# Block 1's key products by feature block, with re-laid first parameters

## The chip, the cores and the metric

The kernel runs on one core of a Trainium2 chip. The metric is the device time of one execution in microseconds, taken as the median of several runs. Beside it stands one profiled execution, whose trace gives every instruction with its start, its duration and what it waited for. Engines: PE is TensorE, with PEld its weight loads; DVE is VectorE, ACT ScalarE, POOL GpSimd, and SP issues the transfers.

## What is computed

Three transformer blocks run over 256 tokens of width 1024: `first_block`, then two blocks of a second model. The part that matters here is the opening of the first one. Two streams, the tokens `x` and a context `ctx`, are normalised and modulated with parameters that come from conditions through a wide matrix, and then projected:

```
sh_a, sc_a, ... = split(silu(c)     @ w_ada + b_ada, 6)      # w_ada: 1024 x 6144
csh_a, csc_a,.. = split(silu(c_ctx) @ w_ada + b_ada, 6)
hc = modulate(rmsnorm(ctx, norm_mix), csh_a, csc_a)          # h * (1 + scale) + shift
hx = modulate(rmsnorm(x,   norm_mix), sh_a,  sc_a)
u  = h @ w_in        # split into qk, v, o, gates, and q, k, v of an attention
```

For the context only keys, values and gates are used; for the tokens all columns. A gated linear recurrence (mLSTM) with four heads and a window attention follow, then an output projection, a feed-forward stage, and the two blocks of the second model, which have parameters of their own (`w_ada_2`).

## The kernel before

All activations lie feature-major: a stream is eight tiles of 128 features by 256 tokens. A product in single precision is made of three fast ones (`mm3`): both operands are split into a rounded `hi` and a rest `lo`, and hi*hi, hi*lo and lo*hi are summed in one accumulation bank (L285 to L287). `load_w` loads 512 KB of weights into a raw tile, casts it to `hi` on ACT (L270) and forms `lo` on DVE or POOL (L273). `proj_fm` makes one 128-feature output block at a time, with the weights stationary and 256 tokens of one stream moving; `proj_tm` makes token-major outputs (values, gates), 272 or 384 columns wide, with the activations stationary.

Work is issued through three lanes, each with its own rings: main (raw tiles `wrm`, five accumulation banks `ppm`), fill (`wrf`, two banks `ppf`) and side (`wra`, two raw tiles, one bank `ppa`). The instructions are written in program order, and a planner orders them when the kernel is built: each engine takes, among what is ready by the planner's own estimate, what comes first in the program. On the chip each engine then keeps that order. SP issues all loads, in one order of its own.

The start runs so. `cond_silu` prepares the conditions. `ada_first` computes shift and scale of both streams in two halves `q` of the feature range, each from eight raw tiles of 512 KB that are borrowed from the three lanes' rings: for each raw tile `ada_mm` (L427) runs four matmuls in four column groups of the array, for both conditions at once. `ada_cols` copies the bank, transposes it in two f32 matmuls against the identity (L435), and two small DVE instructions and a scaling with `norm_mix` finish each half. The streams and the constants are loaded between the raw tiles, after the fourth of them. `rms_bc` squares a stream on ACT (L445, L450), adds on DVE (L448), sums over features with one-column f32 matmuls (L463), takes the root on POOL and spreads the result by f32 matmuls against the identity (L472). `norm_mod` then scales (L516), adds the shift on ACT (L521, L524) and forms `hi` and `lo` per tile of 256 tokens (L522, L523, L525).

`block1` follows: the second value projection with the gates (`win_tm1`, L756 to L759), the early parameters of block 2 (`early`: sixteen raw tiles of `wada20` on the side lane), and then, woven with the gates' chain, four key blocks (`ev_k`: convolution and SiLU), the first value projection (`win_tm0`), the attention's key block (`ev_ka`) and twelve blocks of queries and output gates for the tokens alone (`B1ORD`). The gates' chain begins after four steps of the weave (`pause(4)`); its first matmuls are L851 to L853.

Of the kernel before, what the change touches and what calls it, by code (L numbers as in the profile page):

```python
# [9 lines left out]
F32 = mybir.dt.float32  # L10
# [8 lines left out]
P = 128  # L19
# [5 lines left out]
NKEEP = 5472  # L25
# [3 lines left out]
B1ORD = (*range(9, 13), *range(5, 9), *range(13, 17))  # L29
# [30 lines left out]
for _n, _c in (  # L60
    ("norm_mix", 8), ("norm_ffn", 8), ("final_norm", 8), ("final_norm_w_2", 8),
    ("b_ada", 48), ("b_ada_20", 48), ("b_ada_21", 48),
    ("conv_qk", 32), ("mlstm_norm", 4), ("conv_ffn", 88),
    ("conv_ssd", 48), ("ssd_norm_w", 4), ("ret_gn_w", 4), ("q_norm", 6), ("kv_norm", 2),
    ("gate_b", 16), ("sink", 8), ("dt_bias", 16), ("a_log", 16), ("ssd_d", 8), ("decay", 16), ("iota", 8),
):
    _col(_n, _c)
# [15 lines left out]
def drive(gen):  # L83
    for _ in gen:
        pass
# [76 lines left out]
class Kern:  # L162
# [51 lines left out]
    def load_consts(self):  # L214
        nc = self.nc
        nc.sync.dma_start(self.cols, self.A["cols"])
        nc.sync.dma_start(self.cst, self.A["cst"])
# [6 lines left out]
        nc.vector.tensor_scalar(self.bm[:, 3], self.m["lt"], BIG, None, op0=MUL)  # L224

# [117 lines left out]

    def ada_first(self, W, cond, bcol, mid, use):

        nc, L = self.nc, self.side
        Wv = W[:, 0:2048].rearrange("p (a b) -> p a b", a=2)
        M, F, S = self.main, self.fill, self.side
        for q, raws in enumerate(((M, F, S, M, F, M, S, F), (S, F, S, F, S, F, S, F))):
            ps = L.ps()  # L350
            for k in range(8):
                R = raws[k]
                raw = self.tile([P, 1024], F32, "wr" + R.name, R.raw)
                nc.sync.dma_start(raw.rearrange("p (a b) -> p a b", a=2),
                                  Wv[k * P:(k + 1) * P, :, q * 512:(q + 1) * 512])
                if q == 0 and k == 3:
                    mid()
                self.ada_mm(ps, cond, raw, k)
            pt = self.ada_cols(L, ps)
            b0, _ = COLS[bcol]  # L360
            halves = []
            for a in range(2):
                dst = self.one([P, 2, 4], F32, f"ada_m{q}{a}")
                src = ap_of(pt[:, 64 * a:64 * a + 1], [(1, 2), (32, 2), (128, 2)])
                bo = b0 + 8 * a + 4 * q
                bsrc = ap_of(self.cols[:, bo:bo + 1], [(0, 2), (2, 2), (1, 2)])
                nc.vector.tensor_tensor(dst.rearrange("p c (n j) -> p c n j", j=2), src, bsrc, op=ADD)
                halves.append(dst)
            use(q, *halves)

    def ada(self, W, cond, bcol, out, groups):

        nc, L = self.nc, self.side
        for q in groups:
            ps = L.ps()
            for k in range(8):
                raw = self.tile([P, 1024], F32, "wra", L.raw)
                nc.sync.dma_start(raw, W[k * P:(k + 1) * P, q * 1024:(q + 1) * 1024])
# [60 lines left out]
    def sumsq(self, L, xs):  # L439
# [3 lines left out]
        for i, x in enumerate(xs):  # L443
# [6 lines left out]
            nc.scalar.activation(sq, x, AF.Square)  # L450
# [50 lines left out]
    def norm_mod(self, L, xs, a, sh, out, n=D, slots=None, scale=None):  # L501
# [10 lines left out]
        def start(k):  # L512
            hi, lo = slots(k) if slots else (L.s1(F32R), L.s1(F32R))
            out.append((hi, lo))
            t = L.s1()
            nc.vector.scalar_tensor_tensor(t, xs[k], a[k], bc, op0=MUL, op1=MUL)  # L516
            if sh is None:
                nc.scalar.copy(hi, t)
                return lambda: (nc.gpsimd if k % 2 else nc.vector).tensor_sub(lo, t, hi)
            if k % 2:  # L520
                nc.scalar.activation(t, t, AF.Identity, bias=sh[k])  # L521
                nc.scalar.copy(hi, t)  # L522
                return lambda: nc.gpsimd.tensor_sub(lo, t, hi)  # L523
            nc.scalar.activation(hi, t, AF.Identity, bias=sh[k])  # L524
            return lambda: nc.vector.scalar_tensor_tensor(lo, t, sh[k], hi, op0=ADD, op1=SUB)  # L525
# [187 lines left out]
    def block1(self, xs, hc, hx, ad, early, early2, late):  # L713
# [79 lines left out]
        def ev_x(mb, *a):  # L793
# [892 lines left out]
    def run(self, out, parts=("b1", "l0", "l1")):  # L1686
# [14 lines left out]
        if "b1" in parts:  # L1701
            c1 = self.load_stream("c1T", [M.s2() for _ in range(4)])
            sh, am, hc, hx = [[], []], [[], []], [], []
            norms = [self.norm_mod(M.on(Fl), c1, am[1], sh[1], hc), self.norm_mod(M.on(Fl), xs, am[0], sh[0], hx)]

            def streams():
                self.load_stream("xT", x2)
                self.load_consts()
                for _ in range(3):
                    for g in norms:  # L1710
                        next(g)

            def half(q, a, b):
                for c in range(2):
                    t = self.keep(4)
                    nc.vector.scalar_tensor_tensor(t, b[:, c], 1.0, self.col("norm_mix", 4 * q, 4), op0=ADD, op1=MUL)
                    am[c] += cl(t)
                    sh[c] += cl(a[:, c])

# [198 lines left out]
```

## Time and profile before

| | us |
|---|---|
| median of 3 runs | 1579.48 |
| lowest and highest run | 1576.5 and 1580.1 |
| the profiled execution, device time | 1574.8 |
| its span in the trace | 1573.0 |

The span is the time from the first to the last instruction in the trace; the device time of that execution has 1.8 us more around it. Busy times of TensorE are those of pipelined matmuls, whose ends are modelled, so durations of neighbours overlap; the distance between two starts is what one of them costs in a stream. The granted clock is given as a share of the full 2.4 GHz.

### The profile page before, as it was taken

To read this page: it belongs to the slowest core of one execution; us is meant where nothing else is said; L and a number is where in the kernel's file an instruction comes from. 1 tells how busy PE (TensorE), PEld (TensorE's weight loads), DVE (VectorE), ACT (ScalarE), POOL (GpSimd) and SP (SyncE) were. 2 spreads that over 40 slices of the span, in tenths; PEclk is the share of its full clock that TensorE was granted. 3 is DMA by queue.
4 is the path that set the end of the run, shared out by engine and by line. 5 is a ranking of instruction groups with operands and counts; after the bars stand their busy time and mean duration, and the time that the engine had idled before them with its cause. 6 is when DMAs were issued, how large, how long until landed. Compare 5 with 4: busy or idle time off the path is not lost.

```text
span 1573.0 us, 28294 instructions
## 1 busy us (share of the span) xinstructions
PE 1506.4 (96%) x10518; PEld 1330.7 (85%) x10518; DVE 1133.2 (72%) x2369; ACT 796.1 (51%) x1707; POOL 391.1 (25%) x373
## 2 busy tenths in 40 slices
PE   6899999999999998999999999999998999999997
PEld 3598867879999987888899888888898865899997
DVE  4457588579999946777775348988685775687776
ACT  3444546576545464645464323322366556566563
POOL 0102136231213263476572001101012112010000
PEclk9799999999999997999999999999999999999999
DMA  9856651456777763434245335688443340355663
GB/s 333 276 184 201 229 185 44 134 173 227 246 262 258 244 212 117 127 88 147 80 155 168 94 98 211 213 287 283 153 125 117 95 134 1 95 175 176 186 180 116
DMA packets 81386, 268.49 MB, mean 171 GB/s; under 512 B 9056, under 2 KB 10720, under 8 KB 80992
## 3 DMA queue, kind: packets, MB, share of 16 engines
q1 hardware_dynamic: 80672, 266.16, 52.3%
q8 instruction: 82, 1.34, 0.3%
q10 hardware_dynamic: 576, 0.52, 0.1%
q14 instruction: 56, 0.46, 0.1%
HBM read 265.60 MB, written 1.05 MB: 170 GB/s over the span
## 4 chain that ended last, share of the span: by engine, by line
PE 78%; DVE 8%; issue 6%; DMA 5%; ACT 2%; POOL 1%; SPq 0%; POOLq 0%; DVEq 0%; ACTq 0%
PE t_ppm L285 17%; PE t_ppm L286 17%; PE t_ppm L287 17%; PE t_ppf L285 4%; PE t_ppf L286 4%; PE t_ppf L287 4%; PE t_ppa L427 2%; PE t_ppm L1644 2%; DVE t_wlm L273 1%; PE t_ppm L1048 1%; PE t_ppf L1059 1%; DMA t_wra<-in_wada 1%; DMA t_wrm<-in_wdown 1%; PE t_ppm L1077 1%; PE t_ppm L972 1%
## 5 line engine op out<-in xcount | busy, mean ns | idle before, releaser
L270 ACT CAST t_whm<-t_wrm 128x512 fp32r<-128x512 f32 (+2 forms) x588 | 348.2, 598 | 400.7 <-PE t_ppm L286 308.3
L273 DVE TENSOR_TENSOR t_wlm<-t_wrm,t_whm 128x512 fp32r<-128x512 f32 (+3 forms) x551 | 402.4, 736 | 159.4 <-ACT t_whm L270 153.0
L285 PE MATMUL t_ppm<-t_g1m,t_whm 128*128 128x256 f32 x952 | 271.8, 291 | 0.0
L286 PE MATMUL t_ppm<-t_g1m,t_whm 128*128 128x256 f32 x952 | 269.3, 286 | 0.1
L287 PE MATMUL t_ppm<-t_g1m,t_wlm 128*128 128x256 f32 x952 | 267.4, 285 | 0.8 <-DVE t_wlm L273 0.8
L285 PEld LDWEIGHTS t_ppm<-t_g1m,t_whm 128*128 128x128 f32 x952 | 181.4, 192 | 4.9 <-issue 4.1
L286 PEld LDWEIGHTS t_ppm<-t_g1m,t_whm 128*128 128x128 f32 x952 | 182.3, 192 | 3.7 <-issue 2.8
L287 PEld LDWEIGHTS t_ppm<-t_g1m,t_wlm 128*128 128x128 f32 x952 | 181.4, 192 | 3.4 <-issue 1.7
L273 POOL TENSOR_TENSOR t_wlf<-t_wrf,t_whf 128x512 fp32r<-128x512 f32 (+1 forms) x92 | 118.0, 1291 | 193.9 <-ACT t_whf L270 184.2
L417 DVE SCALAR_TENSOR_TENSOR t_junk<-t_wra,t_sc 128x1024 bf16<-128x1024 f32 x120 | 151.1, 1262 | 18.5 <-DMA t_wra<-in_wada 14.0
L286 PE MATMUL t_ppm<-t_h8m,t_whm 128*128 128x512 f32 (+2 forms) x448 | 159.6, 357 | 1.9 <-DVE t_h8m L525 1.9
L285 PE MATMUL t_ppm<-t_h8m,t_whm 128*128 128x512 f32 (+1 forms) x448 | 158.6, 357 | 2.7 <-ACT t_h8m L524 2.7
L287 PE MATMUL t_ppm<-t_h8m,t_wlm 128*128 128x512 f32 (+2 forms) x448 | 159.2, 357 | 0.0
L270 ACT CAST t_whf<-t_wrf 128x512 fp32r<-128x512 f32 (+2 forms) x148 | 83.3, 574 | 107.3 <-PE t_ppf L286 73.3
L286 PE MATMUL t_ppm<-t_part,t_whm 128*128 128x258 f32 (+1 forms) x400 | 114.0, 285 | 0.0
L287 PE MATMUL t_ppm<-t_part,t_wlm 128*128 128x258 f32 (+1 forms) x400 | 113.6, 284 | 0.0
L285 PE MATMUL t_ppm<-t_part,t_whm 128*128 128x258 f32 (+1 forms) x400 | 113.3, 284 | 0.0
L285 PE MATMUL t_ppm<-t_g2m,t_whm 128*128 128x256 f32 x352 | 98.9, 283 | 0.6 <-ACT t_whm L270 0.5
L287 PE MATMUL t_ppm<-t_g2m,t_wlm 128*128 128x256 f32 x352 | 98.5, 283 | 0.8 <-DVE t_wlm L273 0.8
L286 PE MATMUL t_ppm<-t_g2m,t_whm 128*128 128x256 f32 x352 | 98.6, 282 | 0.0
L286 PEld LDWEIGHTS t_ppm<-t_h8m,t_whm 128*128 128x128 f32 (+1 forms) x448 | 83.9, 187 | 15.4 <-DVE t_h8m L525 2.3
L285 PEld LDWEIGHTS t_ppm<-t_h8m,t_whm 128*128 128x128 f32 x448 | 83.1, 187 | 16.2 <-ACT t_h8m L524 2.9
(542 smaller groups left out, 3521.9 us busy)
## 6 DMA issues: line engine op xcount, KB each, us to landing
t_wrm<-in_wup SPq DMA_DIRECT2D x132, 512.0 KB, 3.7
t_wra<-in_wada SPq DMA_DIRECT2D x102, 512.0 KB, 5.0
t_wrm<-in_w_fm SPq DMA_DIRECT2D x30, 512.0 KB, 3.6
t_wra<-in_wada20t SPq DMA_DIRECT2D x24, 512.0 KB, 4.6
t_wrf<-in_w_fm SPq DMA_DIRECT2D x20, 512.0 KB, 4.7
t_wrf<-in_wd SPq DMA_DIRECT2D x24, 384.0 KB, 3.9
t_wrm<-in_win_fm SPq DMA_DIRECT2D x17, 512.0 KB, 3.6
t_wrm<-in_wdown SPq DMA_DIRECT2D x16, 512.0 KB, 3.9
```

The costliest lines, as they stand in the source:

```text
L270: nc.scalar.copy(hi[:, :c1 - c0], raw[:, c0:c1])
L273: eng.tensor_sub(lo[:, :c1 - c0], raw[:, c0:c1], hi[:, :c1 - c0])
L285: mm(ps, ah, bh, start=start, stop=False)
L286: mm(ps, ah, bl, start=False, stop=False)
L287: mm(ps, al, bh, start=False, stop=stop)
L417: nc.vector.scalar_tensor_tensor(self.tile([P, D], BF16, "junk", 1), raw, 1.0, rows[:, c], op0=MUL, op1=MUL, accum_out=out[:, c, i:i + 1])
L427: self.nc.tensor.matmul(ps[32 * c:32 * c + 32, :T], cond[:, 32 * k:32 * (k + 1)], raw[:, c * T:(c + 1) * T], start=k == 0, stop=k == 7, ti ...
L972: nc.tensor.matmul(po[:, d * T:d * T + 129], Wt[d][c][:, sl], vm[c][:, h], start=i == 0, stop=i == len(keys) - 1)
L1048: nc.tensor.transpose(pp[:, j * T + t * P:j * T + (t + 1) * P], Ps[t][:, c * P:(c + 1) * P], self.m["ident"])
L1059: nc.tensor.matmul(po[j * 64:(j + 1) * 64, :T], v[j][c], pts[j][c // 2][:, (c % 2) * T:(c % 2 + 1) * T], start=c == 0, stop=c == 3, tile_p ...
L1077: nc.tensor.matmul(ps, q[:, t * P:(t + 1) * P], kall, start=True, stop=False)
L1644: nc.tensor.matmul(ps, q, K[0:96, hd], start=True, stop=True)
```

## The change

The first parameters are computed by feature block. The 2048 columns of shift and scale are laid out anew on the host (`wada1s`), so that for each of the eight feature blocks of 128 there are two tiles of 128 x 1024, with rows of 4 KB. `ada_block` runs both through one bank: column group c takes the condition's k = c and k = 4 + c, and two matmuls against a small selecting matrix (`sel`, two columns) sum the four groups and turn the result into columns. The raw tiles have a ring of their own, `wrq`, with five buffers. The weights of the five key blocks (four for the recurrence, one for the attention) are laid out by input feature (`win_k`, 128 x 640 for each).

`front` loads the context and the token stream first, then the column table and the identity. Squares and sums of both streams are formed (part of the second's squares on POOL), one root and four broadcasts serve both. Then, for each feature block k: its parameters, its weights, both streams scaled and split into one operand of 512 columns (`hw`, sixteen buffers), and fifteen products into five banks that stay open over all eight k. The other constants are loaded at k = 1. `block1` gets the five full banks and empties them, then goes on with the value projection as before; the key blocks leave the weave.

```diff
-        nc.sync.dma_start(self.cols, self.A["cols"])
-        nc.sync.dma_start(self.cst, self.A["cst"])
+        nc.sync.dma_start(self.cst[:, P:], self.A["cst"][:, P:])
...
+    def load_first(self):
+        self.nc.sync.dma_start(self.cols, self.A["cols"])
+        self.nc.sync.dma_start(self.cst[:, :P], self.A["cst"][:, :P])
...
-    def ada_first(self, W, cond, bcol, mid, use):
...
+    def ada_block(self, W, cond, bcol, fb, ncol):
         nc, L = self.nc, self.side
+        ps = L.ps()
+        for g in range(2):
+            raw = self.tile([P, 1024], F32, "wrq", 5)
+            nc.sync.dma_start(raw, W[:, g * 1024:(g + 1) * 1024])
+            for c in range(4):
+                k = 4 * g + c
+                nc.tensor.matmul(ps[32 * c:32 * c + 32, :T], cond[:, 32 * k:32 * (k + 1)], raw[:, c * T:(c + 1) * T],
+                                 start=g == 0, stop=g == 1, tile_position=(0, 32 * c))
+        sb = L.s1()
+        nc.vector.tensor_copy(sb, ps[:, :T])
+        pt = self.fill.ps()
+        for j in range(2):
+            nc.tensor.matmul(pt[:, 2 * j:2 * j + 2], sb[:, j * P:(j + 1) * P], self.col("sel", 0, 2), start=True, stop=True)
+        o, _ = COLS[bcol]
+        t, a = self.keep(4), self.keep(2)
+        v = lambda x: x.rearrange("p (j c) -> p j c", j=2)
+        nc.vector.tensor_tensor(v(t), v(pt[:, 0:4]), ap_of(self.cols[:, o + fb:o + fb + 1], [(8, 2), (0, 2)]), op=ADD)
+        nc.vector.scalar_tensor_tensor(a, t[:, 2:4], 1.0, ap_of(self.col(ncol, fb), [(0, 2)]), op0=ADD, op1=MUL)
+        return a, t[:, 0:2]
+
+    def front(self, cond, streams, loads, h):
+        nc, M, Fl, A = self.nc, self.main, self.fill, self.A
+        loads[0]()
+        loads[1]()
+        self.load_first()
+        with self.soon():
+            ps = Fl.ps()
+            for s, xs in enumerate(streams):
+                acc, sq = self.sumsq(M, xs, s)
+                nc.vector.tensor_add(acc, acc, sq)
+                for t in range(2):
+                    nc.tensor.matmul(ps[:, 2 * s + t:2 * s + t + 1], acc[:, t * P:(t + 1) * P], self.ones[:, 0:1],
+                                     start=True, stop=True)
+            v = M.sm(4)
+            nc.vector.tensor_scalar(v, ps[:, 0:4], 1.0 / D, EPS, op0=MUL, op1=ADD)
+            r = self.rsqrt(M, v, 4)
+            bc = Fl.ps()
+            for t in range(4):
+                nc.tensor.matmul(bc[:, t * P:(t + 1) * P], ap_of(r[:, t:t + 1], [(0, P)]), self.m["ident"],
+                                 start=True, stop=True)
+        pss = [M.ps() for _ in range(5)]
+        for k in range(8):
+            a, sh = self.ada_block(A["wada1s"][k], cond, "b_ada", k, "norm_mix")
+            w = self.load_w(M, A["win_k"][k], 640, P)
+            for s, xs in enumerate(streams):
+                sl = slice(s * T, (s + 1) * T)
+                c = 1 - s
+                self.mod_one(M, k, xs[k], a[:, c:c + 1], sh[:, c:c + 1], bc[:, sl], h[k][0][:, sl], h[k][1][:, sl])()
+            if k == 1:
+                self.load_consts()
+            for b in range(5):
+                wh, wl = w(b)
+                self.mm3(pss[b], wh, wl, h[k][0], h[k][1], k == 0, k == 7)
+        return pss
...
-            nc.scalar.activation(sq, x, AF.Square)
+            if pool and i % 3 == 1:
+                nc.gpsimd.tensor_mul(sq, x, x)
+            else:
+                nc.scalar.activation(sq, x, AF.Square)
...
+        rests = [ev_ka(4, s, pss[4][:, s * T:(s + 1) * T]) for s in range(2)]
+        for mb in range(4):
+            for s in range(2):
+                ev_k(mb, s, pss[mb][:, s * T:(s + 1) * T])
         drive(self.proj_tm(L, self.A["win_tm1"], 8, 272, [hc, hx], ev_v1))
+        rests[1]()
...
-            chain(self.proj_fm(L, W, 8, [hc, hx], range(0, 4), ev_k),
-                  self.proj_tm(L, self.A["win_tm0"], 8, 384, [hc, hx], ev_v0),
-                  self.proj_fm(L, W, 8, [hc, hx], [4], ev_ka),
-                  self.proj_fm(L, W, 8, [hx], B1ORD, ev_x)),
+            chain(self.proj_tm(L, self.A["win_tm0"], 8, 384, [hc, hx], ev_v0),
+                  self.proj_fm(L, W, 8, [hx], B1ORD, lambda mb, *a: ev_x(mb + B1BLK, *a))),
             chain(pause(4), self.mlstm_gates(L, gt, gates), adas if ORD == 2 else ())))
...
+            h = [[self.tile([P, 2 * T], F32R, "hw", 16) for _ in range(2)] for _ in range(8)]
```

`mod_one` is the body of the old `norm_mod` for one tile of 256 tokens: a scaling on DVE; then, in even blocks, the shift on ACT straight into `hi` and the rest on DVE, and in odd blocks the shift and the cast in two ACT steps and the rest on POOL. `B1ORD` is renumbered for a weight tensor without the key blocks; its order is the same.

## Rows read from the trace of the kernel before

**Rows 1.** The page: busy time by engine, the clock in 40 slices, costly groups.

```profile
PE 1506.4 (96%) x10518; PEld 1330.7 (85%) x10518; DVE 1133.2 (72%) x2369; ACT 796.1 (51%) x1707; POOL 391.1 (25%) x373
...
PEclk9799999999999997999999999999999999999999
...
L270 ACT CAST t_whm<-t_wrm 128x512 fp32r<-128x512 f32 (+2 forms) x588 | 348.2, 598 | 400.7 <-PE t_ppm L286 308.3
L273 DVE TENSOR_TENSOR t_wlm<-t_wrm,t_whm 128x512 fp32r<-128x512 f32 (+3 forms) x551 | 402.4, 736 | 159.4 <-ACT t_whm L270 153.0
```

**Rows 2.** The page: the chain that ended last, shares by engine.

```profile
PE 78%; DVE 8%; issue 6%; DMA 5%; ACT 2%; POOL 1%; SPq 0%; POOLq 0%; DVEq 0%; ACTq 0%
```

**Rows 3.** Stages: us, busy PE, PEld, DVE, ACT, POOL, granted clock, DMA, GB/s.

```profile
40.00:50.00 10.00, 5.96 (x40) 2.37 (x40) 4.49 (x12) 3.10 (x9) 3.83 (x5) 0.58 0.89 297
62.80:121.00 58.20, 58.14 (x447) 52.21 (x447) 31.96 (x89) 26.67 (x64) 1.88 (x4) 1.00 0.65 203
```

**Rows 4.** The chain of waits, first 160 us: start, us, what.

```profile
4.04 7.39 DMA t_wrf<-in_wada
...
29.52 0.23 PE t_ppm L286
...
45.42 1.12 PE t_ppa L427 x8
...
78.78 0.57 PE t_ppa L427 x8
...
91.80 0.57 PE t_ppa L427 x8
...
120.91 0.22 PE t_ppm L852 x2
...
122.37 0.98 PE t_ppf L463 x8
```

**Rows 5.** Groups of matmuls by line and shape, 62.8 to 121 us.

```profile
L285 PE MATMUL t_ppm<-t_g1m,t_whm 128*128 128x256 f32 x80 | 22.8, 286 | 0.0
...
L427 PE MATMUL t_ppa<-t_wra,t_held 128*32 128x256 f32 x72 | 7.0, 391 | 0.5 <-DMA t_wra<-in_wada 0.5
```

**Rows 6.** TensorE in order of time, first and last of 22, 13 and 27.

```profile
94.83 0.28 PE L286 MATMUL t_ppm<-t_g1m,t_whm 128*128 128x256 f32 x1
...
97.34 0.28 PE L286 MATMUL t_ppm<-t_g1m,t_whm 128*128 128x256 f32 x1
...
107.06 0.33 PE L285 MATMUL t_ppm<-t_whm,t_g1m 128*128 128x384 f32 x1
...
109.14 0.33 PE L285 MATMUL t_ppm<-t_whm,t_g1m 128*128 128x384 f32 x1
...
859.77 0.40 PE L285 MATMUL t_ppm<-t_h8m,t_whm 128*128 128x512 f32 x1
...
865.81 0.39 PE L287 MATMUL t_ppm<-t_h8m,t_wlm 128*128 128x512 f32 x1
```

**Rows 7.** Transfers of the first 42 us, in 40 slices.

```profile
GB/s 0 7 167 210 238 314 334 359 339 298 357 408 392 409 414 413 409 408 406 415 409 402 410 401 403 412 408 430 392 396 406 384 322 166 339 92 222 380 346 254
```

**Rows 8.** Transfers of the first 120 us.

```profile
DMA packets 12282, 31.19 MB, mean 260 GB/s; under 512 B 1392, under 2 KB 1520, under 8 KB 12272
```

**Rows 9.** Groups by line and shape, first 62.8 us: count, busy us, mean ns.

```profile
L525 DVE SCALAR_TENSOR_TENSOR t_g1m<-t_g1m,t_ada_m 128x256 fp32r<-128x256 f32 x7 | 4.7, 671 | 7.1 <-ACT t_g1m L524 7.1
...
L516 DVE SCALAR_TENSOR_TENSOR t_g1m<-t_g2m,t_held,t_ppf 128x256 f32<-128x256 f32 x8 | 3.6, 472 | 0.1
...
L524 ACT ACTIVATE t_g1m<-t_g1m,t_ada_m 128x256 fp32r<-128x256 f32 x7 | 3.5, 504 | 0.0
...
L432 DVE COPY t_g1a<-t_ppa 128x256 f32<-128x256 f32 x2 | 0.8, 424 | 9.7 <-PE t_ppa L427 9.7
```

**Rows 10.** Instructions in order of time, the second stream's scale.

```profile
17.75 1.87 PE L463 MATMUL t_ppf<-t_held,t_g1m 128*128 128x1 f32 x8 [0.56 <-DVE t_g1m L448]
...
21.62 1.23 PE L472 MATMUL t_ppf<-t_held,t_smm 128*128 128x128 f32 x4
```

More of the change, by code (lines that the diff above doesn't have):

```diff
@@ L24 @@
 NFF = 22
-NKEEP = 5472
+NKEEP = 5508
 AH0 = 1
@@ L342, in cond_silu @@
         return o
-    def ada_first(self, W, cond, bcol, mid, use):
+    def ada_block(self, W, cond, bcol, fb, ncol):
         nc, L = self.nc, self.side
[L347 to L369, printed above, removed]
@@ new lines, in mod_one, with ada @@
+    def mod_one(self, L, k, x, a, sh, bc, hi, lo):
+        nc = self.nc
+        t = L.s1()
+        nc.vector.scalar_tensor_tensor(t, x, a, bc, op0=MUL, op1=MUL)
+        if k % 2:
+            nc.scalar.activation(t, t, AF.Identity, bias=sh)
+            nc.scalar.copy(hi, t)
+            return lambda: nc.gpsimd.tensor_sub(lo, t, hi)
+        nc.scalar.activation(hi, t, AF.Identity, bias=sh)
+        return lambda: nc.vector.scalar_tensor_tensor(lo, t, sh, hi, op0=ADD, op1=SUB)
+    def ada(self, W, cond, bcol, out, groups, q0=0):
@@ L377, in ada @@
                 raw = self.tile([P, 1024], F32, "wra", L.raw)
-                nc.sync.dma_start(raw, W[k * P:(k + 1) * P, q * 1024:(q + 1) * 1024])
+                nc.sync.dma_start(raw, W[k * P:(k + 1) * P, (q - q0) * 1024:(q - q0 + 1) * 1024])
                 self.ada_mm(ps, cond, raw, k)
@@ L514, in start @@
             out.append((hi, lo))
+            if sh is not None:
+                return self.mod_one(L, k, xs[k], a[k], sh[k], bc, hi, lo)
             t = L.s1()
             nc.vector.scalar_tensor_tensor(t, xs[k], a[k], bc, op0=MUL, op1=MUL)
[L517 to L525, printed above, removed]
+            nc.scalar.copy(hi, t)
+            return lambda: (nc.gpsimd if k % 2 else nc.vector).tensor_sub(lo, t, hi)
         with self.soon(SOON2):
@@ L710, in swiglu_act, with block1 @@
         return act
-    def block1(self, xs, hc, hx, ad, early, early2, late):
+    def block1(self, xs, hc, hx, pss, ad, early, early2, late):
         nc, L, m = self.nc, self.main, self.m
@@ L1701, in run @@
         if "b1" in parts:
[L1702 to L1718, printed above, removed]
-            self.ada_first(A["wada1"], cond1, "b_ada", streams, half)
-            drive(weave(*norms))
-            self.block1(xs, hc, hx, ads[0], lambda: self.ada(A["wada20"], cond2, "b_ada_20", ads[1], (0, 1)),
-                        lambda: self.ada(A["wada1"], cond1, "b_ada", ads[0], range(2, G1)), late)
+            t4 = [M.s2() for _ in range(4)]
+            c1 = [t[:, i * T:(i + 1) * T] for t in t4 for i in range(2)]
+            h = [[self.tile([P, 2 * T], F32R, "hw", 16) for _ in range(2)] for _ in range(8)]
+            hc, hx = ([(a[:, j * T:(j + 1) * T], b[:, j * T:(j + 1) * T]) for a, b in h] for j in range(2))
+            pss = self.front(cond1, [c1, xs], [lambda: self.load_stream("c1T", t4), lambda: self.load_stream("xT", x2)], h)
+            self.block1(xs, hc, hx, pss, ads[0], lambda: self.ada(A["wada20"], cond2, "b_ada_20", ads[1], (0, 1)),
+                        lambda: self.ada(A["wada1"], cond1, "b_ada", ads[0], range(2, G1), 2), late)
         else:
+            self.load_first()
             self.load_consts()
@@ L1894, in layout @@
     put("iota", np.stack([255 - p, 127 - p, p, 128 + p, p + 1, p + 129, 256 - p, 128 - p], axis=1))
+    sel = (p[:, None] % 32 == np.arange(2)[None]).astype(np.float32)
+    put("sel", sel)
     A["cols"] = cols
```

14 lines of the change are left out of this document (8 added, 6 removed).

## The prediction

> **What bounds the kernel now.** I read the page first, then its chain of waits, then the first 121 us by stages, and only there single instructions. Over the whole span TensorE is busy 96% [rows 1] and 78% of the chain that ended last lies on it [rows 2]. So time saved on TensorE at the start moves everything behind it. The start is the exception: of the 40 clock slices the second, from 39 to 79 us, is one of two at 0.7 [rows 1]. From 40 to 50 us TensorE is busy 5.96 of 10 us at a granted clock of 0.58, a mix of its two levels, 1.2 and 2.4 GHz. From 62.8 to 121 us it is busy 58.14 of 58.20 us at 1.00 [rows 3]. The chain of waits says why: up to 63 us its long pieces are transfers that land late, such as the 7.39 us from 4.04 us on, with short bursts of matmuls between them [rows 4]. What can be won lies ahead of 63 us; after that only less work helps.
>
> **A mark to measure by.** At 120.9 us the gates' matmuls of L852 start [rows 4]. By then the first parameters (16 transfers of 512 KB), the early parameters of block 2 (16 more), both value products and the five key blocks are done, and the other feature blocks follow. The changed kernel must do the same before the same point, so the gain is 120.9 us less the time at which it gets there.
>
> The prices at full clock: a 256-column product starts every (97.34-94.83)/21 = 0.1195 us, a 384-column one every (109.14-107.06)/12 = 0.173 us, a 512-column one every (865.81-859.77)/26 = 0.232 us [rows 6]; a 272-column one lies close to the first, 0.127 us. One raw parameter tile costs 0.57 us, and 1.12 us in the slow stretch; four f32 matmuls of one column cost 0.98 us [rows 4]. As a check on the dense stretch, whose 447 matmuls are 240 key products (80 in each of three lines, one record lost), 96 value products of 384 columns, 72 records of nine raw tiles and some 40 others, most of 272 columns: 240 x 0.1195 + 96 x 0.173 + 9 x 0.57 + 40 x 0.127 = 28.7 + 16.6 + 5.1 + 5.1 = 55.5 us of 58.2 [rows 3, 5]. Some 5% is left over.
>
> **The change, part by part.**
>
> *Streams first.* The two streams (2.1 MB), the columns and the identity (0.3 MB) go ahead of the parameters. Adding up the slices of transfer rate gives 2.1 MB at 9.5 us and 3.8 MB at 14.1 us [rows 7]. The last 1.4 MB of that is the first block's parameters (two 512 KB tiles) and its 328 KB of weights; the next block lands some 3.4 us later. Squares and sums end near 11 us (a square and two adds behind the last tile, each some 0.42 us like the copy of the same size [rows 9]). From the column sums to the broadcast the old kernel took 21.62+1.23-17.75 = 5.1 us for one stream [rows 10]; four broadcasts instead of two add 1.2 us, so the scale is there at 17.3 us. The first parameters: second tile at 13.6 us, 1.1 us of matmul, a copy of 0.42 us, two selecting matmuls of 0.93 us at half rate and two small adds, about 17 us. A pair of scalings (2 x 0.47 us), an ACT step of 0.50 us and hand-overs put the first key product at 19 us.
>
> *Key products by feature block.* 240 products of 256 columns become 120 of 512: 28.7 us become 27.9 us. By the Trainium skill, TensorE: Matmul & The Clock Gate, Part 2 (what happens when you issue a matmul), a stream of 512-column matmuls starts one every 215.7 ns; 120 of them would be 25.9 us and the gain 2 us larger. The trace here shows 232 ns for this very form of product [rows 6], so the measured figure stands.
>
> *Parameters by feature block.* The 16 raw tiles stay 16 raw tiles: 9.1 us at full clock. Four transposes go; 16 selecting matmuls come. They are not in this trace. The nearest rows are the one-column f32 matmuls, 0.245 us each; as a floor I take half a 256-column product, 0.06 us. I take 0.245, 0.49 us for a block. So one block costs TensorE 2 x 0.57 + 0.49 + 15 x 0.232 = 5.1 us, against 3.4 us of transfer: in the new front TensorE, not the queue, sets the pace.
>
> *What the other engines do for one block.* VectorE: copy 0.42, two small adds 0.3, two scalings 0.94, two rests 0.96 to 1.34 in even blocks, weight rests near 0.9 (0.74 for 512 columns [rows 1], and a quarter of that for 128): about 3.6 us. ACT: two to four steps of some 0.5 us and casts of the weights near 0.75: at most 2.8 us [rows 9]. Both fit under 5.1 us.
>
> *The new wait.* Inside a block there is now a chain: selecting matmuls 0.49, two small adds 0.3, two scalings 0.94, ACT 0.50, five hand-overs between engines, each estimated at 0.2 us: 3.2 us before the next block's products may start. Everything behind them on TensorE waits too, since it takes its instructions in order, and all five accumulation banks are held by the open sums, so no other projection can fill in. The next block's parameter matmuls can (1.14 us). Bounds for what stays open at each of seven borders: 0 us if the selecting matmuls run ahead in the gap before the products' second pass, 2.1 us if they come after the last product. In odd blocks the rests go to POOL and ACT has two steps, which leaves such a gap; in even blocks it hardly does. I take 0.9 us, nearer the lower end.
>
> *End of the front.* From 19 us: six parameter blocks not yet done 6.8, seven selections 3.4, 8 x 3.48 = 27.9, the first block's products at half rate 3.0: TensorE dense to 60 us; with seven gaps of 0.9 us, **66.4 us**. Bounds 60 and 75 us.
>
> *What is left from there to the mark.* First value product 96 x 0.127 = 12.2, second 16.6, early parameters 16 x 0.57 = 9.1, the 5% of the check 2.0, gate matmuls and transposes 1.1: 41 us. The emptying of the banks costs little: each takes two convolution steps of about 0.47 us for two streams on VectorE, some 2 us, while one value tile is 24 products = 3 us; I charge 1 us. So the mark comes at 66.4 + 42 = 108.4 us and the gain is 12.5 us. In short, gain = 79 us less the end of the front.
>
> *Nothing in the sum.* The larger ring of parameter tiles and the wide operand tiles cost time only if others lose room; before, the operands took as many bytes as 32 single tiles. Four KB rows instead of two 2 KB pieces: the old transfers already move 392 to 430 GB/s between 12 and 31 us [rows 7]. The loading of the other constants moves behind block 1 and is needed only at the mark; if it were late, the gates would be. The gates start later in the weave, with 7 of the 12 blocks left instead of 12; their chain ends two blocks (5.8 us) before the recurrence needs it. Squares moved to POOL: 3 of 8 for one stream, hidden by the landing.
>
> **Sum.** The profiled execution took 1574.8 us (span 1573.0); less 12.5 is 1562.3 us. That execution lies 4.7 us under the median of the runs, 1579.5, so on that scale the forecast is **1567 us**.
>
> **The rivals.** *Dense front (17%).* The order puts the selections ahead and no gap stays: the front ends at 60 us, gain 19, time 1560.5. For it: one engine's list of ready work fills gaps, as the parameter matmuls do at 78.78 us, among the products [rows 4]. Against: the open banks leave little to fill with.
>
> *Chain exposed (12%).* 2.1 us at each border: front to 75 us, gain 4, time 1575.
>
> *Moved, not saved (8%).* The old kernel moved 31.2 MB by 120 us [rows 8]. The new front needs some 14 MB and can prefetch about 3; the other 14 must cross in 42 us, at 340 GB/s, and the early parameters pass through two buffers: from 78.78 to 91.80 us two pairs came, 6.5 us each [rows 4], which makes 52 us for 16. If the order asks for them sooner, TensorE waits at the head of its queue for up to 0.7 us a tile, 11 us: no gain, 1578. Against: in the dense stretch such waits came to 0.5 us [rows 5], and a tile that is late can slide among the later blocks.
>
> *Front at half clock (13%), the slower side.* From 40 to 50 us a run of matmuls with gaps was granted 0.58 [rows 3]. If the gaps at the borders hold the new front there, a block costs 2 x 1.12 + 0.93 + 15 x 0.433 = 9.7 us (0.433 scaled from 0.23 us for 272 columns [rows 4]), the front ends at 19 + 13.4 + 6.5 + 52 = 91 us and the time is 1579.5 + 12 = 1591.5. The sign turns when the front ends at 79 us, with about six tenths of its work at half rate. Against: at half rate the products outlast the chain, no gap is left, and it was dense work that preceded the rise to 1.00 in the old trace. The Trainium skill, same page, Part 1, says the same way round that the default state is throttled and activity releases it; by that rule this rival ends itself, and the trace agrees (1.00 throughout the dense stretch [rows 3]).
>
> **Numbers.** 0.2% (3.2 us) is about what can be told from no change. The main case holds 50%. Main, dense and exposed cases end faster: 79%. Moved-not-saved is the same: 8%. Half clock is slower: 13%. Later stages are ordered anew, for which I allow 4 us either way. The likeliest case alone spans 1562 to 1572; eight in ten reach from the dense front with a lucky order, 1552, to a front that saves nothing, 1583.
>
> **What will show it.** Right: key products from about 19 us, 512 columns wide, at a granted clock of 1.00 from 30 us; the last near 66 us; the gates' first matmuls near 108 us; after that the same distances as before. Wrong: products that wait for ACT or VectorE by 2 us or more at each border, 0.43 us pitches past 30 us, parameter transfers at the end of TensorE's waits after the front, or a stage behind the mark that grew.

## The result: slower by 1.4%

| | before | after |
|---|---|---|
| median of the runs | 1577.99 us (4 runs, 1574.15 to 1580.1) | 1597.68 us (4 runs, 1592.86 to 1606.89) |
| ratio, 95% interval | | 1.0142 [1.0121, 1.0163] |
| profiled execution | 1574.8 us | 1606.89 us, the slowest of the four |

The forecast was 1567 us, the range ended at 1583, and slower had 13%. The time lies outside the range on the wrong side of no change. (The two medians are 1.25% apart; the ratio is an estimate of its own, with its interval.) The profiled execution of the new kernel is 9 us above its median, so the losses by stages below are upper figures. In its profile all lines have moved down: L285 to L287 are now L290 to L292, L427 is L478 (and L359 in the front), L852 is L905. First its page, to be read against [rows 1, 2]:

```profile
PE 1517.0 (95%) x10418; PEld 1335.1 (83%) x10418; DVE 1138.9 (71%) x2390; ACT 792.7 (49%) x1710; POOL 391.0 (24%) x375
...
PEclk9989999999999998899999999999999999999999
...
PE 69%; DVE 12%; DMA 9%; issue 6%; POOL 2%; ACT 2%; SPq 0%; POOLq 0%; DVEq 0%; ACTq 0%
PE t_ppm L290 16%; PE t_ppm L291 15%; PE t_ppm L292 15%; DMA t_wra<-in_wada 6%; PE t_ppf L292 3%; PE t_ppf L290 3%; PE t_ppf L291 3%; DVE t_wlm L278 3%; DVE t_junk L468 2%; PE t_ppm L1697 2%; PE t_ppm L1101 1%; PE t_ppa L478 1%; PE t_ppf L1112 1%; PE t_ppm L1130 1%; DMA t_wrm<-in_wup 1%
```

TensorE's share of the chain fell from 78 to 69%, and one kind of transfer, the side lane's parameters (`t_wra<-in_wada`), holds 6% of it. Next TensorE by stages, the kernel before and then the one after; columns: length, busy time, granted clock, DMA share, GB/s.

```profile
0.00:60.00 60.00, 38.36 (x262) 0.80 0.89 310
60.00:180.00 120.00, 118.59 (x952) 1.00 0.66 214
180.00:310.00 130.00, 126.46 (x952) 0.99 0.42 134
310.00:780.00 470.00, 447.83 (x3454) 0.97 0.56 182
780.00:1280.00 500.00, 493.57 (x2804) 0.99 0.51 166
```

```profile
0.00:60.00 60.00, 43.65 (x274) 1.00 0.79 287
60.00:180.00 120.00, 108.69 (x799) 0.93 0.66 213
180.00:310.00 130.00, 122.68 (x896) 0.96 0.40 126
310.00:780.00 470.00, 443.75 (x3372) 0.96 0.56 182
780.00:1280.00 500.00, 485.36 (x2747) 0.99 0.49 160
```

Let lost time be the length less busy time times clock: it counts idle time and the half of the work at half rate. For the first 60 us the clock column needs care. It shows 1.00 from the start, but the rows show both fronts at half rate there: in the new one five 512-column products took 2.43 us at 25.44 and 1.36 us at 31.80 (next chain), in the old one a raw tile took 1.06 us at 23.63 and 0.64 us at 25.50. So the front is taken in stretches, the kernel before and then the one after:

```profile
0.00:24.50 24.50, 12.87 (x80) 1.00 0.92 328
24.50:35.00 10.50, 7.92 (x54) 0.67 1.00 386
35.00:42.00 7.00, 4.59 (x53) 0.97 0.86 264
42.00:60.00 18.00, 12.99 (x82) 0.54 0.80 260
```

```profile
0.00:30.00 30.00, 15.52 (x75) 1.00 0.92 339
30.00:60.00 30.00, 28.13 (x201) 1.00 0.65 234
```

With the first stretch of each at half rate, the first 60 us lost 60 - 12.87/2 - 7.92 x 0.67 - 4.59 x 0.97 - 12.99 x 0.54 = 36.8 us before and 60 - 15.52/2 - 28.13 = 24.1 after: the front gave **12.7 us**, where 12.5 was forecast. Then 60 to 180 us lost 1.4 before and 18.9 after, 180 to 310 us 4.8 and 12.2, 310 to 780 us 35.6 and 44.0, 780 to 1280 us 11.4 and 19.5 (the clock is given to two places, which leaves some 2 us open in the two long stages). The gain is there, and is more than paid back. How it goes, in the chain of waits after the front (start, us, what):

```profile
25.44 2.43 PE t_ppm L290 x5
...
31.80 1.36 PE t_ppm L290 x5
...
59.72 0.98 PE t_ppa L478 x10
...
70.05 4.38 DMA t_wra<-in_wada
74.47 0.68 PE t_ppa L478 x8
75.17 4.09 DMA t_wra<-in_wada
79.31 0.68 PE t_ppa L478 x8
81.78 4.58 DMA t_c<-in_c2T
88.95 0.57 PE t_ppm L290
...
152.50 4.19 DMA t_wra<-in_wada
```

and TensorE in order of time at the first of these stalls:

```profile
71.99 0.64 PE L478 MATMUL t_ppa<-t_wra,t_held 128*32 128x256 f32 x8
74.47 0.64 PE L478 MATMUL t_ppa<-t_wra,t_held 128*32 128x256 f32 x8 [1.85 <-DMA t_wra<-in_wada]
75.04 0.39 PE L290 MATMUL t_ppm<-t_whm,t_hw 128*128 128x272 f32 x1
```

The value products (272 columns) are ready and stand behind an early parameter tile of block 2 whose transfer has not landed. Stages of 10 us, columns as above:

```profile
50.00:60.00 10.00, 10.00 (x78) 1.00 0.23 73
60.00:70.00 10.00, 10.00 (x63) 1.00 0.64 207
70.00:80.00 10.00, 6.54 (x62) 1.00 0.66 201
80.00:90.00 10.00, 6.02 (x38) 0.73 0.88 284
90.00:100.00 10.00, 10.00 (x69) 0.76 0.70 217
```

From 50 to 60 us the queue moves only 73 GB/s. What SP issued, in order of time:

```profile
17.58 1.59 SPq L429 DMA_DIRECT2D t_wra<-in_wada  x2
...
54.36 5.33 SPq L268 DMA_DIRECT2D t_wrm<-in_win_tm  x2
60.35 4.99 SPq L429 DMA_DIRECT2D t_wra<-in_wada  x2
```

The side ring's two raw tiles were loaded at 17.6 us, and the third early tile could be asked for only when TensorE had read the first, at 60.3 us. From 48 to 59.4 us SP itself stands at two loads of weights (L268), until VectorE has read their raw tiles; over 40 to 62 us it waits 17.4 us there and 0.6 us at the side ring. Then TensorE waits, and the clock falls. The stall at 81.78 us is another one: the transfer of the second model's context.

### The profile page after: what moved, and what is told of

Its sections match the earlier page's. It is cut to its first block, busy times and chain, and to the rows that moved or that the text cites. A ratio compares the mean times of both kernels' runs of the same rounds, so it can differ in the third digit from the quotient of the medians.

```text
span 1605.1 us, 28167 instructions
## 1 busy us (share of the span) xinstructions
PE 1517.0 (95%) x10418; PEld 1335.1 (83%) x10418; DVE 1138.9 (71%) x2390; ACT 792.7 (49%) x1710; POOL 391.0 (24%) x375
## 4 chain that ended last, share of the span: by engine, by line
PE 69%; DVE 12%; DMA 9%; issue 6%; POOL 2%; ACT 2%; SPq 0%; POOLq 0%; DVEq 0%; ACTq 0%
PE t_ppm L290 16%; PE t_ppm L291 15%; PE t_ppm L292 15%; DMA t_wra<-in_wada 6%; PE t_ppf L292 3%; PE t_ppf L290 3%; PE t_ppf L291 3%; DVE t_wlm L278 3%; DVE t_junk L468 2%; PE t_ppm L1697 2%; PE t_ppm L1101 1%; PE t_ppa L478 1%; PE t_ppf L1112 1%; PE t_ppm L1130 1%; DMA t_wrm<-in_wup 1%
## 5 line engine op out<-in xcount | busy, mean ns | idle before, releaser
L278 DVE TENSOR_TENSOR t_wlm<-t_wrm,t_whm 128x512 fp32r<-128x512 f32 (+4 forms) x557 | 400.8, 725 | 185.3 <-ACT t_whm L275 171.8
L290 PE MATMUL t_ppm<-t_g1m,t_whm 128*128 128x256 f32 x776 | 222.9, 293 | 1.9 <-ACT t_whm L275 1.8
L291 PE MATMUL t_ppm<-t_g1m,t_whm 128*128 128x256 f32 x776 | 221.0, 288 | 0.2
L292 PE MATMUL t_ppm<-t_g1m,t_wlm 128*128 128x256 f32 x776 | 218.8, 287 | 1.0 <-DVE t_wlm L278 1.0
L468 DVE SCALAR_TENSOR_TENSOR t_junk<-t_wra,t_sc 128x1024 bf16<-128x1024 f32 x120 | 152.4, 1273 | 25.8 <-DMA t_wra<-in_wada 21.6
L292 PE MATMUL t_ppm<-t_h8m,t_wlm 128*128 128x512 f32 (+2 forms) x448 | 160.7, 360 | 2.7 <-DVE t_wlm L278 2.7
L290 PE MATMUL t_ppm<-t_h8m,t_whm 128*128 128x512 f32 (+1 forms) x448 | 159.6, 359 | 2.7 <-ACT t_h8m L419 2.7
L290 PEld LDWEIGHTS t_ppm<-t_g1m,t_whm 128*128 128x128 f32 x776 | 149.2, 194 | 6.3 <-ACT t_whm L275 2.7
L291 PEld LDWEIGHTS t_ppm<-t_g1m,t_whm 128*128 128x128 f32 x776 | 150.1, 194 | 2.8 <-issue 1.4
L292 PEld LDWEIGHTS t_ppm<-t_g1m,t_wlm 128*128 128x128 f32 x776 | 149.5, 194 | 2.7 <-DVE t_wlm L278 1.8
L290 PE MATMUL t_ppm<-t_part,t_whm 128*128 128x258 f32 (+1 forms) x400 | 113.0, 283 | 0.0
L292 PE MATMUL t_ppm<-t_part,t_wlm 128*128 128x258 f32 (+1 forms) x400 | 113.0, 283 | 0.0
L292 PE MATMUL t_ppm<-t_g2m,t_wlm 128*128 128x256 f32 x352 | 99.0, 283 | 2.7 <-DVE t_wlm L278 2.7
L290 PE MATMUL t_ppm<-t_g2m,t_whm 128*128 128x256 f32 x352 | 99.2, 283 | 0.3 <-ACT t_whm L275 0.3
L292 PEld LDWEIGHTS t_ppm<-t_h8m,t_wlm 128*128 128x128 f32 (+1 forms) x448 | 84.1, 188 | 17.8 <-DVE t_wlm L278 4.6
L290 PEld LDWEIGHTS t_ppm<-t_h8m,t_whm 128*128 128x128 f32 x448 | 83.7, 188 | 16.5 <-ACT t_h8m L419 2.8
```

The lines of the kernel that those rows point to most:

```text
L278: eng.tensor_sub(lo[:, :c1 - c0], raw[:, c0:c1], hi[:, :c1 - c0])
L290: mm(ps, ah, bh, start=start, stop=False)
L291: mm(ps, ah, bl, start=False, stop=False)
L292: mm(ps, al, bh, start=False, stop=stop)
L468: nc.vector.scalar_tensor_tensor(self.tile([P, D], BF16, "junk", 1), raw, 1.0, rows[:, c], op0=MUL, op1=MUL, accum_out=out[:, c, i:i + 1])
```

## The experiments

Theory A: the sixteen early tiles (and the later ones) starve in a side ring of two raw tiles. Once the old front had hidden eight of them where TensorE had nothing else to do; now all come from 59.7 us on, and TensorE stands at their matmuls. Theory B, the rival: any change of the program's order moves the later stages by 10 to 20 us. Theory C: the new rings take room from others. The expectations count 30 us of such waits; that sum takes the waits of weight loads and of matmuls together. TensorE's matmuls alone stood 13.3 us for `t_wra` from 63 to 640 us, in 8 waits, against 0.5 us before.

**Load one raw tile in eight.** In both kernels:

```diff
-                raw = self.tile([P, 1024], F32, "wra", L.raw)
-                nc.sync.dma_start(raw, ...)
+                if k == 0:
+                    raw = self.tile([P, 1024], F32, "wra", L.raw)
+                    nc.sync.dma_start(raw, ...)
```

> This leaves out part of the computation: of each group of eight raw parameter tiles on the side lane only the first is loaded, and all eight matmul sets use it (the groups of block 2 computed early, those of block 1's later parameters, and one more before block 2). The matmuls stay. Theory A (TensorE stands at the head of its queue until raw tiles of the two-buffer ring land: 13.1 + 9.8 + 7.1 = 30 us of such waits after the front in the changed kernel): nearly all of those waits go, and the time falls by 25 to 35 us, to 1563 to 1573. Theory B (every edit orders the later stages anew, and the loss is the luck of that order): 1580 to 1605, waits moved elsewhere. Theory C (the new rings take room from others): no change beyond 1%.

> The same omission in the kernel before: of each group of eight raw tiles on the side lane only the first is loaded. Theory A: behind the first 63 us such waits came to 0.5 us there, but the early tiles were taken during the starved front, so their matmuls move at most a few us: 1570 to 1580, and the changed kernel with the same omission is then 5 to 20 us faster than this one. Theory B: anything between 1565 and 1595, and no order between the two.

Measured: 1566.39 us, ratio 0.9927 [0.9905, 0.9948], for the new kernel, 31 us less than it; 1561.91 us, ratio 0.9898 [0.9870, 0.9926], for the old. The first is as theory A has it. The second missed: without these loads the old kernel gains 14.5 us too and is the faster of the two. One reason is likely that its front waited for transfers, and part of what the new front avoids is this traffic: from 24 to 60 us its TensorE is busy 29.70 us at 0.81, in place of 26.00 at 0.67. The other is a stage far behind, to which the section on places comes: there after_one_raw took 506.1 us and before_one_raw 495.6.

**Early tiles through the front's ring of five.**

```diff
-    def ada(self, W, cond, bcol, out, groups, q0=0):
+    def ada(self, W, cond, bcol, out, groups, q0=0, ring=("wra", 2)):
...
-                raw = self.tile([P, 1024], F32, "wra", L.raw)
+                raw = self.tile([P, 1024], F32, *ring)
...
-  lambda: self.ada(A["wada20"], cond2, "b_ada_20", ads[1], (0, 1)),
+  lambda: self.ada(A["wada20"], cond2, "b_ada_20", ads[1], (0, 1), 0, ("wrq", 5)),
```

> The sixteen early tiles of block 2 go through the ring of five that the front leaves free; the later parameters keep the two-buffer ring. Theory A: the 13.1 us of waits between 60 and 180 us and the fall of the clock behind them go, those of 180 to 300 us may stay or shrink: 1575 to 1588. Theory B: 1585 to 1605 as likely as lower.

Measured: 1571.10 us, ratio 0.9959 [0.9941, 0.9977], 26.6 us less than the changed kernel. From 50 to 60 us the queue now moves 297 GB/s, and 60 to 180 us lose 4.0 us in place of 18.9 (116.03 of 120 busy at 1.00), 180 to 310 us 6.2 in place of 12.2 (125.05 of 130 at 0.99). So some 21 of the 26.6 us lie where the waits were. But the edit also changed the order: the second model's context comes to its matmuls of L1241 at 181 us and of L1319 at 260 us (old numbering), in place of 230 and 322 in the changed kernel and 220 and 310 in the old one. The last run below comes back to this.

**A null control.** `B1ORD` of the old kernel permuted to 5 to 16 in rising order.

> Control for theory B: the kernel before with the query blocks of the recurrence ahead of those of the attention; same work, another order. Theory A: within 6 us of before, 1572 to 1584. Theory B: a change of 10 to 20 us either way from an edit that changes no work.

Measured: 1580.73 us, ratio 1.0030 [1.0012, 1.0049]. As a rule for any edit theory B falls: this one is worth 5 us, not 20. That no order is worth as much is not shown, and the last run below is one that cost 19 us.

**A second cause: places.** In three new kernels with quite different traffic (after, after_one_raw, after_early_wrq) the last parameter stage, from the last matmul of L1527 (now L1580) to the first of L1644 (now L1697), took 504.9, 506.1 and 504.4 us, and 495.4 and 495.6 in before and before_one_raw. The order of instructions in that stage is the same in the three and in before, on every engine (before_one_raw has some 60 of its matmuls elsewhere). What differs is in the built program: where the tiles lie. The ring `wra` declares two raw tiles, but they are given places in memory only after the order is fixed, and a load waits for the reader of its own place. Counted in the built programs, the loads whose place was last used two or three loads before (block 1's tiles are 24, in the old kernel 30 with the six that its front borrows):

```
                        block 1's tiles      block 3's 48 tiles
                        two     three        two     three
before                    6      19            7      37
after                    19       2           45       1
after_late_three         24       0            6      36
before_late_two           4      19           47       0
before_early_two         28       0            6      36
after_ring_three          0      19            0      37
after_early_wrq          18       2           46       0
after_wrq_late_three     22       0            6      36
before_early_ring5        6      19            8      36
```

The old kernel had a third place by the luck of its layout; the new one lost it. SP's waits in that stage, before and after (us, times, longest):

```profile
SPq L263 <- DVE t_wlm L273: 287.5, 78, 12.8
SPq L263 <- DVE t_wlf L273: 52.9, 18, 8.9
SPq L411 <- DVE t_junk L417: 24.5, 20, 4.8
```

```profile
SPq L268 <- DVE t_wlm L278: 219.3, 74, 13.0
SPq L462 <- DVE t_junk L468: 66.0, 41, 4.8
SPq L268 <- DVE t_wlf L278: 57.6, 22, 7.4
SPq L462 <- DMA t_wra<-in_wada: 21.2, 22, 2.6
```

SP issues in order. In 41 loads instead of 20 it stands until VectorE has read the tile, and the weights' loads stand behind it. VectorE's waits for these tiles rise from 14.0 to 21.6 us, and TensorE waits for rests of weights: 5.2 us (`t_wlm`, `t_wlf`) in place of 1.3. The chain that ended last says it most clearly: in this stage transfers into `t_wra` hold 10.8% of it in after, 7.0 in after_early_wrq, 6.7 in after_one_raw and 8.4 in before_late_two (below), the four whose stage took 501 us or more. In every other kernel here the 200 longest pieces of the chain hold none over 2 us, and the stage took 495 to 499 us. A tile that is made eight floats wider, with only its first 1024 columns used, is placed elsewhere. That moves the third place about. The edit is

```diff
-                raw = self.tile([P, 1024], F32, "wra", L.raw)
+                raw = self.tile([P, 1024 + 8], F32, "wra", L.raw)[:, :1024]
```

in `ada` (after_late_three and before_early_two), and in `ada_dve` (before_late_two)

```diff
-            raw = self.tile([P, D], F32, "wra", self.side.raw)
+            raw = self.tile([P, D + 8], F32, "wra", self.side.raw)[:, :D]
```

> The new kernel, with the tiles of ada() eight floats (32 bytes) wider and only their first 1024 columns used. All engines issue the same instructions in the same order as in the new kernel; only places in memory change. In the last parameter stage (48 tiles of the third block, read by VectorE) a load then takes a place that was used three loads before in 36 of 48 cases; in the new kernel it was two loads before in 45 of 48, in the old kernel three before in 37 of 48. Theory 'third place' (the side ring declares two buffers, but the placement had given the old kernel three places, and a load waits for the reader of its place): the stage between 805 and 1309 us shrinks by the 9 us by which it had grown, and the time falls from 1598 to about 1588. Rival 'other phase' (the stage grew because transfers and VectorE meet in another order in time): no change, 1594 to 1601.

> The old kernel, with the tiles of the parameters that VectorE reads (ada_dve) eight floats wider. In the last stage a load then takes the place of two loads before in 47 of 48 cases (three before in 37 of 48 in the old kernel). Some of the order between 200 and 600 us changes with it. 'Third place': 6 to 10 us slower than before, 1583 to 1588, with the loss between 778 and 1273 us. Rival 'other phase': 1574 to 1580.

> The old kernel, with the tiles of ada() eight floats wider: the same order on every engine as in the run before_late_two, but here the last stage keeps its third place (36 of 48) and the early parameters lose theirs: the 24 later tiles of block 1's parameters take the place of two loads before in all cases, where 19 were three before. If the starved parameter matmuls after the front (30 us in the new kernel, 0.5 us in the old between 63 and 175 us) come from the lost third place, this is 8 to 20 us slower than before, 1585 to 1597. If they come from moving the sixteen early tiles behind the front, as theory A has it, under 4 us: 1576 to 1581.

Measured. after_late_three: 1596.98 us, 1.0116 [1.0083, 1.0150]; the stage took 498.2 us instead of 504.9, and SP's waits there are those of before:

```profile
SPq L268 <- DVE t_wlm L278: 267.5, 73, 14.7
SPq L268 <- DVE t_wlf L278: 61.2, 19, 7.8
SPq L462 <- DVE t_junk L468: 25.3, 22, 4.8
```

The stage is nearly as the theory has it (in before_order, where SP stands at 20 loads as in the old kernel, it took 498.6 us too), but the whole time is not told apart from the changed kernel's and misses the 1588 expected. before_late_two: 1587.87 us, 1.0074 [1.0044, 1.0104], the stage 501.6 us: slower as expected, with 64.9 us of SP's waits in 42 loads. before_early_two: 1585.04 us, 1.0048 [1.0031, 1.0065], the stage unchanged at 495.4. These two programs have the same order on every engine and differ in places alone; from the old kernel both differ in order too, between 200 and 600 us. So the early places are to be read between the two: before_early_two is 2 us behind before_late_two at the first matmul of L1319 (310.7 and 308.2 us), 5 us at that of L1448 (609.0 and 603.7) and 6 us at the start of the last stage (786.2 and 779.9), where the late places give it all back (1281.6 and 1281.5). The early places count as well, but not where they were expected.

**Three raw tiles declared.** `Lane(self, "a", 2, ...)` becomes `Lane(self, "a", 3, ...)`, in either kernel:

> The new kernel with three raw buffers declared for the side lane instead of two; loads then take a place of three loads before almost everywhere. Theory A with the third place: the starved waits of the parameter matmuls (30 us) mostly go and the last stage loses its 9 us: 1562 to 1575, at or below the run with the early tiles in the five-buffer ring (1571). If a third buffer cannot cover a tile that is asked for as soon as the front ends, 1580 to 1590.

> The old kernel with three raw buffers declared for the side lane, as in the run after_ring_three; all later parameter loads take a place of three loads before. If places in memory alone decide, 3 to 8 us faster than before (the last stage had 8 of 48 loads at two, the middle ones nearly all): 1568 to 1574. If the old order already hides its waits, 1574 to 1580.

Measured: 1586.97 us, 1.0056 [1.0037, 1.0075], and 1577.40 us, 1.0011 [0.9997, 1.0025]. In the new kernel a third tile gives back 11 us, as its second case has it: from 60 to 180 us TensorE still waits for `t_wra` eight times, 7.2 us. Its last stage took 499.0 us, though SP stands there at 38 of the loads (58.3 us): the count of SP's waits is no sure sign by itself, the chain is. The old kernel gains nothing.

**Both repairs, and the same ring for the old kernel.** after_wrq_late_three is after_early_wrq with `1024 + 8` for the tiles that stay in `wra`; its order is that of after_early_wrq on every engine.

> The new kernel with both repairs: the sixteen early tiles go through the five-buffer ring of the front, and the tiles of ada() that stay on the side ring are eight floats wider, so that the last parameter stage has its third place (36 of 48 loads). If the two causes add, this is the 1571 us of the run after_early_wrq less the 6.5 us by which the third place shortened the last stage: 1562 to 1568. If the last stage's gain is taken back behind it, as it partly was in the run after_late_three, 1568 to 1573.

> The old kernel, with its sixteen early tiles in a ring of their own with five buffers, as in the run after_early_wrq; the last stage keeps its third place. What separates this kernel from after_wrq_late_three is the front itself. If the front is worth the 12 to 14 us by which it loses less time in the first 60 us, this one takes 1574 to 1582 us: in the old front the queue is the limit, and more buffers bring nothing. If the ring was the whole of what after_early_wrq gained, 1563 to 1570.

Measured: **1564.08 us**, ratio 0.9924 [0.9905, 0.9944], in the first case; it is faster than both kernels. The old kernel with the same ring for its early tiles: 1576.98 us, 1.0008 [0.9991, 1.0025]. Stages of after_wrq_late_three:

```profile
0.00:60.00 60.00, 42.73 (x264) 1.00 0.90 322
60.00:180.00 120.00, 116.15 (x914) 0.99 0.66 219
180.00:310.00 130.00, 124.89 (x930) 1.00 0.42 129
310.00:780.00 470.00, 444.43 (x3489) 0.98 0.57 183
780.00:1280.00 500.00, 490.18 (x2748) 0.99 0.52 168
```

Lost: 24.9 (15.20 us busy ahead of 30.6 us taken at half rate), 5.0, 5.1, 34.5 and 14.7 us. The front keeps its gain, and the next two stages lose little more than before.

**The stall behind the second model's context**, 4.58 us at 81.78 us above: its stream loaded one parameter group later (`load_c(ads[1][:, 0, 8:16])` for `0:8`), on top of both repairs.

> As the run after_wrq_late_three, and in addition the second model's context is loaded behind the second early parameter group instead of the first, so that ACT's squares for it stand later in ACT's order and no longer wait for their transfer ahead of the emptying of the five open banks. If that stall (4 to 6 us of TensorE between 73 and 90 us) sets the end, 3 to 6 us less than that run; if what is moved fills a gap that would else be empty, no change or up to 4 us more.

Measured: 1583.01 us, 1.0044 [1.0027, 1.0061], 19 us slower. The wait for `t_c` goes, but at 75.79 us the chain waits 5.91 us for an early tile instead. And the context's way through block 2 falls behind: its matmuls of L1241 begin at 221 us in place of 182, those of L1319 at 310 in place of 260. That is where the old kernel has them (220 and 310), and with them there this kernel is slower than the old one. So the run does not tell what that stall is worth alone; it suggests that the early context, which came with the ring of five as a change of order, carries part of what that ring brought. With the context late, 60 to 180 us lose 9.6 us and 180 to 310 us 6.1 (111.48 and 125.16 us busy at 0.99), 15.7 together where the changed kernel loses 31.1: about 15 us are gone in this order too. Why the whole is 19 us slower was not tried further.

## Why the prediction was wrong

The front itself came out as worked: 12.5 us forecast, 12.7 by lost time. For before_early_ring5 and after_wrq_late_three the same count gives 37.5 - 24.9 = 12.6 us; of the former 19.75 us are busy ahead of 36.0 us at half rate, then 3.89 at 0.99, 8.13 at 0.50 and 4.74 at 0.99. Between these two kernels the whole times differ by 1576.98 - 1564.08 = 12.9 us as well; since they also differ in where the second model's context runs, that is no second proof. Single steps of that sum were off and cancelled, which is luck.

- *First key product at 19 us*: 25.4. The last token tile's square starts at 13.25 us, behind its transfer, the sums end at 15.3 (11 forecast), the root is done at 18.95 and the broadcasts run to 21.1 (17.3 forecast).
- *Seven borders of 0.9 us*: 1.9 us in all (42.13 of the 44.00 us from 25.4 to 69.4 us are busy), in two waits of selecting matmuls for a copy. The last 512-column product ends at 69.4 us, but three early tiles (24 records, eight to a tile, 0.98 + 0.56 + 0.57 = 2.1 us) stand among the products. So the products and their parameters took 69.4 - 25.4 - 2.1 - 1.9 = 40.0 us, where the dense front had 41; without the three tiles the front ends at 67.3, and 66.4 was forecast.
- *Front at half clock*: only to 30 us, as the main case had it (the first block's products at half rate, 1.00 from 30 us on).
- *Early parameters, 16 x 0.57 = 9.1 us*: **this step failed.** It charged their work and nothing for their transfers. In the old kernel eight of them had started by 63 us, while TensorE was starved anyway; the dense stretch showed 0.5 us of waits [rows 5] because only the rest was left to it. In the new kernel TensorE comes to one every 2.2 to 2.6 us from 69.4 to 79.3 us, a place's next load is issued only when its tile was read, and it takes over 4 us to land; the ring had not run ahead during the front. The rival *Moved, not saved* named this wait, but priced it at up to 11 us and gave it 8%. What the runs show: TensorE's matmuls stood 13.3 us for `t_wra`, the chain up to 640 us has eight of these transfers over 4 us (at 70, 75, 153, 198, 215, 223, 562 and 574 us), and the clock fell behind several of them (0.73 from 80 to 90 us, 0.83 from 150 to 160, 0.76 from 230 to 240, 0.85 from 580 to 590). From 60 to 310 us the new kernel lost 25 us more than the old one. The ring of five took 26.6 us off its time, some 21 of them in this stretch, and 15 also with the context late. The transfers from 153 us on are past the sixteenth tile (its matmuls run at 112.3 us): later parameters, on the same ring.
- *Nothing in the sum: the larger ring and the wide operands cost time only if others lose room*: others lost room. The side ring's third place went, and that is 1571.10 - 1564.08 = 7.0 us at the same order, most of it in a stage that begins 700 us after the change. It could not be read from the trace of before, which shows no places.
- *The mark at 108.4 us*: 137.6, and 131.2 with both repairs. Five of the twelve blocks that followed the gates before now come ahead of them, 120 products or 14.3 us; the prediction says so (7 of 12 left) and did not add them, so its own mark lies at 122.7. The first matmul of the recurrence (L939, now L992) came at 174.2 before, at 179.6 after, and at 173.8 us with both repairs.
- *Emptying of the banks, 1 us*: one wait of 2.9 us, behind the context's transfer at 81.78 us, which the sum did not have.
- *4 us either way for later stages*: too little by half; 310 to 780 and 780 to 1280 us each lost some 8 us more, in the profiled execution.

From 1576.98 us (the old kernel with a ring of five), then: the new front -12.9, the lost place +7.0, the starved early tiles +26.6, which is 1597.7. This is three differences between runs, which add up by themselves; only the second is between programs of one order, and the first and the third both take in, with opposite signs, what the early context is worth.

Open: how much of the 26.6 us is the early context, how much is the lost place of block 1's tiles, which in the old kernel cost some 6 us (before_early_two against before_late_two), and why after_late_three gave back little in whole time while its stage shrank by 6.7 us.

## What to carry to other kernels

Work that is moved out of a starved stretch takes its transfers along: ask which ring they go through and whether it can run ahead during the stretch that is now dense, before charging only their instructions. If the engine in question takes its instructions in order, a ring's next tile stalls all that is ready behind it. And a change of buffers can cost in a distant stage where not one instruction has changed; count how far back each load's place was last used, before and after. Where an edit lets a planner order the program anew, compare when the large pieces start before crediting the edit with the whole difference.

## What the runs showed of the hardware

Both kernels ran their first matmuls at half rate, where the clock column shows 1.00: in the new front 512-column products started every 0.427 us up to 29.4 us and every 0.23 us from 30.4 us on. At the start of these traces the distance between starts tells the rate, not the column. The old front fell back, to 0.54 from 42 to 60 us, with 12.99 of 18 us busy; the new one stayed at 1.00 from 30 to 81 us. Then 10 us with 6.54 busy came at 1.00, 10 us with 6.02 busy at 0.73 and 10 us without a gap at 0.76, so with two stretches of some 4 us idle another 6.02 x 0.27 + 10.00 x 0.24 = 4 us went to the clock. The Trainium skill, TensorE: Matmul & The Clock Gate, Part 1 (HAM oscillation), says that transfers which are not hidden let the clock fall and so cost twice; the trace agrees, with those two values.

Two programs with the same instructions in the same order on every engine took 1571.10 and 1564.08 us (ratios 0.9959 and 0.9924): places in memory alone moved a program by some 0.4%.
